# Streaming conformer step on one core: gate-row modulation weights and third taps moved into block 0's attention, more work on ScalarE, zero-padded low part of q in block 0's scores

## The chip, the cores and the metric

One core of one Trainium2 chip runs the whole layer as one program. The metric is the device time of one execution in microseconds. The kernel before takes 1776.56 us, the median of three runs (1776.23 to 1776.82). A profile shows one execution by engine: PE (TensorE, with its weight loads as PEld), DVE (VectorE), ACT (ScalarE), POOL (GpSimd) and SP (SyncE, which here only issues DMAs).

## The reference

One layer over 2048 prompt frames and 32 sample frames, model width 1024, in fp32. In short:

```python
mod = c @ w_mod + b_mod
shift, scale, gate = jnp.split(mod, 3, axis=-1)
h = rms_norm(x, g_pre) * (1 + scale[:, None, :]) + shift[:, None, :]
z = h @ w_in
a, b, z_conv, q, k, v, z_attn, g_conv, g_attn = jnp.split(z, cuts, axis=-1)
u = a * jax.nn.sigmoid(b)
# A: 31-tap causal depthwise convolution of u, LayerNorm over 512 channels
y = jax.nn.silu(layer_norm(y, ln_g, ln_b)) * jax.nn.silu(z_conv)
y_conv = y @ w_conv_out
# B: 8 heads of 64, every 64-frame chunk sees itself and the 8 chunks before
s = q.k * 64 ** -0.5 + bias;  p = softmax(s);  o = p.v
y_attn = (o * jax.nn.silu(z_attn)) @ w_attn_out
merged = sigmoid(g_conv) * y_conv + sigmoid(g_attn) * y_attn
out = rms_norm(merged @ w_o, g_post)
return x + gate[:, None, :] * out
```

The sample frames run the same layer with cached rows in front. `gate` depends on `c` alone, not on a frame; it enters only in the last line.

## The kernel before

**Tiles and blocks.** The prompt is worked in four blocks of 512 frames; block 0 carries the 32 sample frames too, so its rows are 544 wide and its projections come as two halves of 272. Every fp32 operand is split into a high and a low part, and a product is three matmuls (`mm3`: high by high, low by high, high by low). A block has three stretches: the attention (projections of q, k, a, b and the z gates from a list, `FILL`, woven between the score, transpose and value matmuls of 24 units of one pair of heads, one head and one part of the queries); the tail (the two gate projections `C_GC` and `C_GA`, output tile `pj`, and the attention's out projection, `py<-ah`); and the rest (`co`, the convolution's out projection, `py<-cohi`, then `w_o`).

**Weights.** `plan` lists the weight pieces in the order of use, half a megabyte each. `weights()` hands out piece i and splits piece i+2 (ACT copies the high part, L226; DVE or POOL subtracts the low part, L228), has SP load piece i+4 into one of two `raw` buffers, and has ACT issue the 1 MB DMA that keeps piece i+1 in DRAM for the later blocks (L236). Later blocks load the split pieces instead.

**Gate rows.** The eight pieces of `w_mod` for `gate` stand in block 0's tail, one after each pair of gate projections. `gate_rows` loads `b_mod` and `g_post`, accumulates four pieces in one PSUM tile `pm` (L153, four matmuls a piece) and starts `gate_row`, whose `pg` (L583) spreads the row; two DVE operations later it goes to DRAM as `gp_d`, from where the end of the block loads it (`gp`, `gps`).

**Convolution.** The 31 taps of the four channel tiles are 124 DVE operations on `y` a block, taken from one generator, `pace.idle`. In block 0's attention `pace.pump` takes them at fixed places of a unit (`TP`: one at the first, one at the second and none at the third); the others run in the tail, where `pace.tick` takes one whenever the planner's DVE time is at most its PE time plus a lead. After the last tap comes the LayerNorm: `u` sums on POOL, `pmean` twice on PE, rsqrt on DVE, then in `co` the tanh on ACT and `xn` on DVE, and `cohi` and `colo`, which the first `py<-cohi` needs.

**Order.** All engines work in the order written. The planner `Pace` counts PE and DVE time by its own prices and so decides where started tasks and taps are emitted; `on_v` at L227 decides whether DVE or POOL subtracts a low part: DVE for the `mod` pieces, in block 0's tail (`pace.dense`), and where there are no taps left and DVE is ahead.

**Scores.** For a head of 64 rows the high part of q is stored on all 128 rows with the other head's keys' rows (`qh`); its low part `ql` is on 64 rows in block 0, and on 128 rows with zeros in the blocks after it.

Of the kernel before, what the change touches and what calls it, by code (L numbers as in the profile page):

```python
# [8 lines left out]
F32 = mybir.dt.float32  # L9
F32R = mybir.dt.float32r  # L10
# [24 lines left out]
NIN = 5632  # L35
BIG = 1e30
# [9 lines left out]
TP = (1, 1, 0)  # L46
# [5 lines left out]
def FILL(b):  # L52

    part = dict(q=C_Q, k=C_K, a=C_A, b=C_B, z=C_ZA, c=C_ZC)
# [84 lines left out]
def mixer_kernel(ctx, tc, x_prompt, x_sample, c_prompt, c_sample, cache_conv, cache_k, cache_v,  # L139
# [175 lines left out]
    def h_stats(pool, b, xs):  # L315
# [12 lines left out]
        V.tensor_scalar(ss, ss, 1.0 / D, EPS, op0=OP.mult, op1=OP.add)  # L328
# [152 lines left out]
    conv_ready, ln_done = set(), {}  # L481
# [78 lines left out]
    def mod_rows(n, dst):  # L560
        pm = ps.tile([P, 512], F32, tag="T", name="pm", bufs=2)
        for kp in range(KT // 2):
            wh, wl = weights(("mod", 2 * kp, n * 512))
            for kk in range(2):
                k = 2 * kp + kk
                mm(pm[0:4], c4[:, k, :], wh[:, kk, :], k == 0, False)
                mm(pm[0:4], c4[:, k, :], wl[:, kk, :], False, k == KT - 1)
                yield
        V.tensor_copy(dst, pm[0:4])

    def gate_rows(tmp):

        for n in range(2):
            m4, bg = tmp("m4")[0:4, 0:512], tmp("bg")
            bm, gr = bg[0:2, 0:512], bg[0:2, 512:1024]
            nc.sync.dma_start(bm, dram(b_mod, 2 * D + n * 512, [[0, 2], [1, 512]]))
            nc.sync.dma_start(gr, dram(g_post, n * 512, [[0, 2], [1, 512]]))
            yield from mod_rows(4 + n, m4)
            pace.start(gate_row(n, m4, bm, gr), 4.0)

    def gate_row(n, m4, bm, gr):
        pg = pp_tile("pg")
        nc.tensor.matmul(pg[0:2], lhsT=sel, rhs=m4, start=True, stop=True)  # L583
        V.tensor_tensor(bm, pg[0:2], bm, op=OP.add)
        V.tensor_tensor(bm, bm, gr, op=OP.mult)
        nc.sync.dma_start(gp_d[:, n * 512:(n + 1) * 512], bm)
        yield 0.0
# [31 lines left out]
    with tc.tile_pool(name="init", bufs=1) as ini:  # L619
# [64 lines left out]
        with tc.tile_pool(name="x0", bufs=5) as x0:  # L684
# [37 lines left out]
            V.tensor_scalar(ss, ss, 1.0 / D, EPS, op0=OP.mult, op1=OP.add)  # L722
# [74 lines left out]
    for b in range(NB):  # L797
        NT, YW, ypieces = shape(b)
        PTW = 896 if b == 0 else 1280
        TW = TB + TS if b == 0 else 640  # L800
        LA = 2 if b == 0 else 1

        with tc.tile_pool(name="at", bufs=1) as at:
            def tmp(name):
                return at.tile([P, NT], F32, tag="tmp", name=name, bufs=3)
# [29 lines left out]
            if b == 1:  # L835

# [607 lines left out]
```

## Time and profile before

| | us |
|---|---|
| median of three runs | 1776.56 |
| profiled execution | 1774.66 |
| its span | 1772.9 |
| PE busy in the span | 1690.7 (95%) |
| DVE busy | 1154.7 (65%) |
| ACT busy | 597.5 (34%) |
| POOL busy | 212.1 (12%) |

The profiled execution is 1.9 us under the median and 1.8 us longer than its span. PE's share says that the kernel is mostly matmul; it is an average, and the 82 us without PE lie in a few places. In forty slices of the span, the eleventh (443 to 487 us, the end of block 0's tail) has PE busy at half and its granted clock at 0.6 of full; all other slices after the start show 8 or 9 tenths.

### The profile page before, as it was taken

What the parts mean: (1) busy time and instruction counts of PE and PEld (TensorE: products, weight loads), DVE (VectorE), ACT (ScalarE), POOL (GpSimd) and SP (SyncE); (2) the same over time, 40 slices, a digit from 0 to 9 for tenths busy, and PEclk for the clock granted to TensorE, in tenths of its full rate; (3) what the DMA queues carried; (4) which work ended last, traced back from release to release, by engine and by line L of the source; (5) the groups of instructions that cost most, each with busy time, mean ns of one, the idle gap of its engine ahead of it and who ended that gap; (6) DMA issues with size and microseconds to landing.
All of it is one profiled execution on the core that took longest, in us unless ns stands there. A gap on an engine that the chain in (4) does not pass through costs nothing.

```text
span 1772.9 us, 23618 instructions
## 1 busy us (share of the span) xinstructions
PE 1690.7 (95%) x9221; PEld 1430.4 (81%) x9221; DVE 1154.7 (65%) x2119; ACT 597.5 (34%) x1156; POOL 212.1 (12%) x163
## 2 busy tenths in 40 slices
PE   6889999989499999999899999999999999999997
PEld 4778899988388788888788888888888888888886
DVE  6556876887855957775652967765652967766523
ACT  5345454233331245531220035531320045531211
POOL 4322222002220000001120000001120000000120
PEclk9999999999699999999999999999999999999999
DMA  8796565767375684465465585455565574445553
GB/s 267 216 326 207 189 215 202 272 229 262 132 255 196 243 305 174 156 221 190 150 217 188 196 307 188 140 198 210 181 218 191 199 272 144 171 167 201 190 190 143
DMA packets 132326, 368.61 MB, mean 208 GB/s; under 512 B 9326, under 2 KB 75050, under 8 KB 101975
## 3 DMA queue, kind: packets, MB, share of 16 engines
q1 hardware_dynamic: 123575, 304.19, 50.1%
q10 hardware_dynamic: 8640, 62.92, 8.7%
q8 instruction: 73, 1.20, 0.3%
q14 instruction: 38, 0.31, 0.1%
HBM read 280.41 MB, written 91.77 MB: 210 GB/s over the span
## 4 chain that ended last, share of the span: by engine, by line
PE 78%; DVE 8%; DMA 4%; ACT 2%; issue 1%; ACTq 0%; POOL 0%; DVEq 0%; SPq 0%; POOLq 0%
PE pj L153 44%; PE py L153 8%; PE pv L153 4%; PE sps L153 4%; PE pt L157 4%; PE op L153 3%; PE oT L153 3%; PE oS L153 3%; PE oP L153 1%; DVE y L134 1%; DVE w L134 1%; PE vS L153 1%; PE vT L153 1%; DMA raw<-in_w_attn_out_dram 1%; DMA raw<-in_w_in_dram 1%
## 5 line engine op out<-in xcount | busy, mean ns | idle before, releaser
L153 PE MATMUL pj<-hh,w 128*128 128x512 f32 (+1 forms) x4800 | 974.7, 357 | 11.9 <-DVE kk L134 6.1
L153 PEld LDWEIGHTS pj<-hh,w 128*128 128x128 f32 x4800 | 778.4, 189 | 133.2 <-issue 8.9
L134 DVE SCALAR_TENSOR_TENSOR y<-u,dww,y 128x512 f32<-128x512 f32 (+1 forms) x480 | 338.2, 770 | 0.4
L1073 ACT ACTIVATE sp<-sp,mn 128x640 f32<-128x640 f32 (+5 forms) x136 | 103.7, 762 | 112.5 <-DVE mn L134 112.3
L1108 ACT ACTIVATE pth<-pt 128x256 fp32r<-128x256 f32 (+4 forms) x184 | 91.9, 501 | 135.8 <-PE pt L157 129.3
L134 DVE TENSOR_TENSOR ptl<-pt,pth 128x256 fp32r<-128x256 f32 (+4 forms) x184 | 104.2, 567 | 27.2 <-ACT pth L1108 25.4
L134 DVE CUSTOM_DVE_ANT_0 sp<-sps,bias 128x640 f32<-128x640 f32 (+4 forms) x128 | 94.4, 737 | 29.6 <-PE sps L153 28.1
L153 PE MATMUL py<-cohi,w 128*128 128x512 f32 (+1 forms) x320 | 93.5, 366 | 19.2 <-ACT cohi L1260 17.7
L226 ACT ACTIVATE w<-raw 128x1024 fp32r<-128x1024 f32 x72 | 75.6, 1054 | 89.1 <-DMA raw<-in_w_mod_dram 18.6
L153 PE MATMUL py<-ah,w 128*128 128x512 f32 (+1 forms) x480 | 96.3, 356 | 8.3 <-DVE t L134 7.1
L153 PEld LDWEIGHTS py<-ah,w 128*128 128x128 f32 x480 | 80.1, 192 | 23.5 <-DVE t L134 7.5
L157 PE MATMUL pt<-ident,sp 128*128 128x128 f32 (+1 forms) x600 | 94.2, 272 | 0.0
L228 POOL TENSOR_TENSOR w<-raw,w 128x1024 fp32r<-128x1024 f32 x30 | 73.3, 2443 | 170.5 <-ACT w L226 142.8
L528 POOL TENSOR_TENSOR u<-y 128x512 f32<-128x512 f32 (+1 forms) x4 | 6.3, 1581 | 671.4 <-DVE y L134 671.4
L153 PEld LDWEIGHTS py<-cohi,w 128*128 128x128 f32 x320 | 58.8, 195 | 29.0 <-ACT cohi L1260 19.1
L134 DVE TENSOR_SCALAR sp<-sp,ll 128x640 f32<-128x640 f32 (+5 forms) x136 | 75.6, 556 | 4.8
L134 DVE TENSOR_TENSOR w<-raw,w 128x1024 fp32r<-128x1024 f32 x42 | 53.3, 1278 | 31.5 <-ACT w L226 31.0
L153 PE MATMUL sps<-kk,qh 128*128 128x320 f32 (+1 forms) x224 | 69.2, 316 | 3.3 <-DVE kk L134 2.0
L157 PEld LDWEIGHTS pt<-ident,sp 128*128 128x128 f32 (+1 forms) x600 | 68.8, 140 | 3.9 <-issue 1.3
L153 PE MATMUL sps<-kk,ql 128*128 128x320 f32 (+1 forms) x224 | 70.8, 323 | 0.0
L1344 POOL TENSOR_TENSOR mg<-mg,t 128x512 f32<-128x512 f32 (+1 forms) x32 | 46.4, 1451 | 168.7 <-issue 114.0
L134 DVE SCALAR_TENSOR_TENSOR t<-t,py 128x512 f32<-128x512 f32 (+1 forms) x40 | 23.2, 584 | 59.3 <-PE py L153 59.2
(247 smaller groups left out, 2224.8 us busy)
## 6 DMA issues: line engine op xcount, KB each, us to landing
w<-kept SPq DMA_DIRECT2D x176, 1024.0 KB
kept<-w ACTq DMA_DIRECT2D x60, 1024.0 KB
raw<-in_w_in_dram SPq DMA_DIRECT2D x48, 512.0 KB
bias<-bias_d SPq DMA_DIRECT2D x32, 320.0 KB
xt<-in_x_prompt_dram SPq DMA_DIRECT2D x16, 512.0 KB
wm<-in_w_mod_dram SPq DMA_DIRECT2D x16, 512.0 KB
xr<-in_x_prompt_dram SPq DMA_DIRECT2D x16, 512.0 KB
vs_d<-vcur SPq DMA_DIRECT2D x12, 512.0 KB
```

What stands on the lines that cost most here:

```text
L134: return fn(out, *a, **k)
L153: nc.tensor.matmul(out, lhsT=lhsT, rhs=rhs, start=start, stop=stop)
L157: nc.tensor.transpose(out, in_, idn)
L226: act(wh, raw, AF.Copy)
L228: (V if on_v else G).tensor_tensor(wl, raw, wh.bitcast(F32), op=OP.subtract)
L528: G.tensor_tensor(s2[:, 0:YW], Y[2][:, 0:YW], Y[3][:, 0:YW], op=OP.add)
L1073: self.ex[i] = lambda: act(sp[0:m, 0:nk], sp[0:m, 0:nk], AF.Exp, bias=mn[0:m], scale=-1.0, accum_out=ll[0:m])
L1108: act(self.ph[0:r, f0:f1], pt[0:r, o:o + f1 - f0], AF.Copy)
L1344: G.tensor_tensor(mg, mg, t2, op=OP.add)
```

## The change

It touches block 0 most. The eight gate pieces move from the tail's list into the attention's (`m0` to `m7` of `FILL`); each has a PSUM tile of its own, and ACT (first piece) or DVE (the others) adds it to a row in `aof`. `TP` takes a third tap in each unit. `ql` gets 128 rows with zeros in block 0 too. The second form of `h` (`hf`) and the LayerNorm's `xn` are computed by ACT instead of DVE; rsqrt has nine DVE operations instead of eleven, and the division by the width goes into the squares' scale. Scores tiles `sp` become parts of one row, and `tmp` has two buffers instead of three in block 0. The low part of a `mod` piece is now subtracted by whichever engine the planner's rule picks.

```diff
-TP = (1, 1, 0)
+TP = (1, 1, 1)
...
-    order = "b0 a0 q1 k1 b1 a1 b2 q2 k2 a2 z0 b3 a3 z1 q3 k3 z2 z3 c0 c1 c2 c3" if b == 0 else \
+    order = "b0 a0 q1 m0 k1 m1 b1 m2 a1 m3 b2 q2 m4 k2 m5 a2 m6 z0 m7 b3 a3 z1 q3 k3 z2 z3 c0 c1 c2 c3" if b == 0 else \
...
-                on_v = key[0] == "mod" or pace.dense or pace.idle is None and pace.dve <= pace.pe + DV
+                on_v = pace.dense or pace.idle is None and pace.dve <= pace.pe + DV
...
-    def rsqrt(y, x, xh, t, iters=3):
+    def rsqrt(y, x, t, u):
         V.tensor_scalar(y.bitcast(I32), x.bitcast(I32), -0.5, 1597463007.0, op0=OP.mult, op1=OP.add)
-        V.tensor_scalar(xh, x, -0.5, None, op0=OP.mult)
-        for _ in range(iters):
-            V.tensor_tensor(t, y, y, op=OP.mult)
-            V.tensor_tensor(t, t, xh, op=OP.mult)
-            V.scalar_tensor_tensor(y, t, 1.5, y, op0=OP.add, op1=OP.mult)
+        V.scalar_tensor_tensor(t, y, -0.5, y, op0=OP.mult, op1=OP.mult)
+        V.tensor_tensor(t, t, x, op=OP.mult)
+        V.scalar_tensor_tensor(y, t, 1.5, y, op0=OP.add, op1=OP.mult)
+        V.tensor_tensor(t, y, y, op=OP.mult)
+        V.tensor_tensor(t, t, x, op=OP.mult)
+        V.tensor_scalar(u, t, 0.375, -1.25, op0=OP.mult, op1=OP.add)
+        V.tensor_tensor(u, u, t, op=OP.mult)
+        V.scalar_tensor_tensor(y, u, 1.875, y, op0=OP.add, op1=OP.mult)
...
-        V.tensor_scalar(hf, src, Gm[:, w, ct:ct + 1], Sh[:, w, ct:ct + 1], op0=OP.mult, op1=OP.add)
+        act(hf, src, AF.Identity, scale=Gm[:, w, ct:ct + 1], bias=Sh[:, w, ct:ct + 1])
...
+    def mod_part(i):
+        n, kp = i // 4, i % 4
+        m4, bm, gr = aof[0:4, 3, 0:512], aof[0:2, 2, 0:512], aof[0:2, 1, 0:512]
+        if kp == 0:
             nc.sync.dma_start(bm, dram(b_mod, 2 * D + n * 512, [[0, 2], [1, 512]]))
             nc.sync.dma_start(gr, dram(g_post, n * 512, [[0, 2], [1, 512]]))
+        wh, wl = weights(("mod", 2 * kp, (4 + n) * 512))
+        pm = pp_tile("pm")
+        for kk in range(2):
+            mm(pm[0:4], c4[:, 2 * kp + kk, :], wh[:, kk, :], kk == 0, False)
+            mm(pm[0:4], c4[:, 2 * kp + kk, :], wl[:, kk, :], False, kk == 1)
+            yield
+        if kp == 0:
+            act(m4, pm[0:4], AF.Copy)
+        else:
+            V.tensor_tensor(m4, pm[0:4], m4, op=OP.add)
+        if kp == 3:
+            pace.start(gate_row(n, m4, bm, gr), 1.5)
...
-                return at.tile([P, NT], F32, tag="tmp", name=name, bufs=3)
+                return at.tile([P, NT], F32, tag="tmp", name=name, bufs=2 if b == 0 else 3)
...
-            if b == 1:
+            if b < 2:
+                qls.clear()
                 for _ in range(2):
-                    qls.append(wp.tile([P, 2, TB], F32R, tag="raw", name="ql0"))
+                    qls.append(wp.tile([P, 2, TB], F32R, tag="raw", name="ql0") if b else
+                               at.tile([P, 2, NT], F32R, tag="ql", name="ql", bufs=2))
                     G.memset(qls[-1][64:128, 0].bitcast(F32), 0.0)
                     G.memset(qls[-1][0:64, 1].bitcast(F32), 0.0)
...
                 mm(out, qh[:, s, q0:q0 + m], kk[:, s, k0:k1], True, False)
-                if b == 0:
-                    mm(out, ql[r, q0:q0 + m], kk[r, s, k0:k1], False, True)
-                else:
-                    mm(out, ql[:, s, q0:q0 + m], kk[:, s, k0:k1], False, True)
+                mm(out, ql[:, s, q0:q0 + m], kk[:, s, k0:k1], False, True)
...
-            rate = (88.0 if b == 0 else 62.0) / sum(loads)
+            rate = (95.0 if b == 0 else 62.0) / sum(loads)
...
-                        V.tensor_scalar(xn[ct][:, o0:o1], Y[ct][:, a0:a1], vecs[:, 44 + ct:45 + ct],
-                                        vecs[:, 48 + ct:49 + ct], op0=OP.mult, op1=OP.add)
+                        act(xn[ct][:, o0:o1], Y[ct][:, a0:a1], AF.Identity, scale=vecs[:, 44 + ct:45 + ct],
+                            bias=vecs[:, 48 + ct:49 + ct])
```

PE in block 0's tail, the stretch that ends in `co`. `pj` are the gate projections, `py<-ah` the attention's out projection, `pm` and `pg` the gate rows, `pmean` the LayerNorm's sums and `pxt` the transposes of the next block's input. Before, its last rows:

```order
L153 MATMUL pmean<-lnlo,onesr 128x32
L153 MATMUL pj<-hh,w 128x272 x3
L153 MATMUL pm<-w,c_91 4x512 x4
L153 MATMUL py<-ah,w 128x272 x48
L153 MATMUL pm<-w,c_91 4x512 x4
L583 MATMUL pg<-m_4460,sel 2x512
L153 MATMUL pmean<-lnhi,onesr 128x512
L153 MATMUL pmean<-lnlo,onesr 128x512
L153 MATMUL pmean<-lnhi,onesr 128x32
L153 MATMUL pmean<-lnlo,onesr 128x32
L157 MATMUL pxt<-ident,xt 128x128 x4
L153 MATMUL py<-cohi,w 128x272
```

and the changed kernel's PE in the same tail, from the first `pmean` group on:

```order
L155 MATMUL pmean<-lnlo,onesr 128x32
L155 MATMUL pj<-hh,w 128x272 x15
L155 MATMUL py<-ah,w 128x272 x48
L155 MATMUL pj<-hh,w 128x272 x45
L155 MATMUL pmean<-lnhi,onesr 128x512
L155 MATMUL pmean<-lnlo,onesr 128x512
L155 MATMUL pmean<-lnhi,onesr 128x32
L155 MATMUL pmean<-lnlo,onesr 128x32
L155 MATMUL pj<-hh,w 128x272 x147
L155 MATMUL py<-ah,w 128x272 x48
L159 MATMUL pxt<-ident,xt 128x128 x4
L155 MATMUL py<-cohi,w 128x272
```

Before, only the four transposes stand between the second `pmean` group and the first `py<-cohi`; now 147 `pj` and 48 `py<-ah` do, and `pm` and `pg` are gone from the tail.

DVE at the start of that tail, up to the first operation on a `py<-ah` (`t`). `ah` is the attention's output split, `w<-raw` the subtraction of a weight's low part, `y` a tap. Before:

```order
L134 TENSOR_TENSOR ah<-aof,ah 128x544 x4
L134 TENSOR_TENSOR w<-raw,w 128x1024
L134 SCALAR_TENSOR_TENSOR y<-u,dww,y 128x574 x3
L134 TENSOR_TENSOR w<-raw,w 128x1024
L134 SCALAR_TENSOR_TENSOR y<-u,dww,y 128x574 x6
L134 TENSOR_TENSOR w<-raw,w 128x1024
L134 SCALAR_TENSOR_TENSOR y<-u,dww,y 128x574 x2
L134 TENSOR_SCALAR y<-u,dww,vecs 128x574
L134 SCALAR_TENSOR_TENSOR y<-u,dww,y 128x574 x3
L134 TENSOR_TENSOR w<-raw,w 128x1024
L134 SCALAR_TENSOR_TENSOR y<-u,dww,y 128x574 x6
L134 TENSOR_TENSOR w<-raw,w 128x1024 x2
```

and DVE at the same place of the changed kernel:

```order
L136 TENSOR_TENSOR ah<-aof,ah 128x544 x4
L136 TENSOR_TENSOR w<-raw,w 128x1024
L136 SCALAR_TENSOR_TENSOR y<-u,dww,y 128x574 x2
L136 TENSOR_TENSOR w<-raw,w 128x1024
L136 SCALAR_TENSOR_TENSOR y<-u,dww,y 128x574 x6
L136 TENSOR_TENSOR w<-raw,w 128x1024
L136 SCALAR_TENSOR_TENSOR y<-u,dww,y 128x574 x6
L136 TENSOR_TENSOR w<-raw,w 128x1024
L136 TENSOR_SCALAR y<-u,dww,vecs 128x574
L136 SCALAR_TENSOR_TENSOR y<-u,dww,y 128x574 x6
L136 TENSOR_TENSOR w<-raw,w 128x1024
L136 SCALAR_TENSOR_TENSOR t_3576<-t_3576,py 128x272
```

The number of taps ahead of `t` is the same, 21; one of six subtractions is gone.

## Rows read from the trace of the kernel before

**Rows 1.** PE's waits, 310 to 500 us: engine, line, releaser, total us, times, longest.

```profile
PE py L153 <- ACT cohi L1260: 17.7, 4, 13.8
PE py L153 <- DVE t L134: 7.1, 2, 6.2
...
PE py L153 <- DVE mg L134: 1.0, 2, 0.5
PE pxt L157 <- DVE hf L134: 0.7, 1, 0.7
```

**Rows 2.** PE's timeline, block 0's tail: start, busy us, work, count, [idle before].

```profile
300.26 24.32 PE L153 MATMUL pj<-hh,w 128*128 128x272 f32 x192
324.42 1.09 PE L153 MATMUL pm<-w,c 128*4 128x512 f32 x4
325.35 4.67 PE L153 MATMUL py<-ah,w 128*128 128x272 f32 x36
...
369.98 3.09 PE L153 MATMUL py<-ah,w 128*128 128x272 f32 x12 [6.22 <-DVE t L134]
...
446.55 0.80 PE L153 MATMUL pmean<-lnhi,onesr 128*128 128x512 f32 x1
...
462.79 0.59 PE L153 MATMUL py<-cohi,w 128*128 128x272 f32 x1 [13.82 <-ACT cohi L1260]
...
476.25 0.64 PE L157 MATMUL pxt<-ident,xt 128*128 128x128 f32 x4
```

**Rows 3.** PE's timeline at scores: block 0 (256 to 268 us), then block 1.

```profile
256.89 0.40 PE L153 MATMUL sps<-kk,qh 128*128 128x512 f32 x1
...
257.65 3.26 PE L153 MATMUL pj<-hh,w 128*128 128x272 f32 x24
260.75 0.40 PE L153 MATMUL sa<-kk,qh 128*32 128x512 f32 x1
...
261.68 0.55 PE L157 MATMUL pt<-ident,sp 128*128 128x128 f32 x3
...
267.48 0.22 PE L153 MATMUL sps<-kk,qh 128*128 128x128 f32 x1
...
267.89 0.66 PE L157 MATMUL pt<-ident,sp 128*128 128x128 f32 x4
...
705.02 0.31 PE L153 MATMUL sps<-kk,qh 128*128 128x320 f32 x1
...
705.32 0.31 PE L153 MATMUL sps<-kk,qh 128*128 128x320 f32 x1
```

**Rows 4.** Stretches: us, then busy us (instructions) by engine, PE clock, DMA share, GB/s.

```profile
core 0: us, PE busy (x) PEld busy (x) DVE busy (x) ACT busy (x) POOL busy (x), PEclk, DMA share, GB/s
111.40:286.30 174.90, 171.46 (x1285) 154.28 (x1284) 129.91 (x309) 89.30 (x216) 49.12 (x24) 1.00 0.61 212
...
205.78:228.66 22.88, 22.88 (x172) 20.45 (x173) 18.71 (x41) 10.23 (x26) 7.31 (x4) 1.00 0.56 199
300.26:370.00 69.74, 62.42 (x482) 60.00 (x481) 56.81 (x73) 21.30 (x34) 1.92 (x1) 0.98 0.77 268
```

**Rows 5.** Groups by form: attention (two rows, 100 to 300), tail (two, 300 to 432).

```profile
L228 POOL TENSOR_TENSOR w<-raw,w 128x1024 fp32r<-128x1024 f32 x22 | 54.2, 2463 | 139.8 <-ACT w L226 112.2 <-DMA kept<-w 7.5 <-DMA raw<-in_w_in_dram 5.3
L134 DVE SCALAR_TENSOR_TENSOR y<-u,dww,y 128x574 f32<-128x574 f32 x40 | 36.2, 906 | 0.1
...
L134 DVE SCALAR_TENSOR_TENSOR y<-u,dww,y 128x574 f32<-128x574 f32 x80 | 60.8, 812 | 0.3
L134 DVE TENSOR_TENSOR w<-raw,w 128x1024 fp32r<-128x1024 f32 x25 | 31.6, 1272 | 23.7 <-ACT w L226 23.2 <-issue 0.4
```

**Rows 6.** ACT's waits, 300 to 448 us.

```profile
ACT w L226 <- DMA raw<-in_w_mod_dram: 18.6, 3, 7.1
```

**Rows 7.** PE's longest wait on DVE before 310 us, and ACT's timeline ahead of it.

```profile
PE pj L153 <- DVE kk L134: 6.1, 1, 6.1
...
95.67 0.39 ACT L855 ACTIVATE kk<-pj 64x272 fp32r<-64x272 f32 x1 [5.58 <-DMA bias_d<-msk]
```

**Rows 8.** PE's longest wait after 500 us.

```profile
PE pj L153 <- DVE t L134: 4.5, 1, 4.5
```

More of the change, by code (lines that the diff above doesn't have):

```diff
@@ L35 @@
 NIN = 5632
+C_MOD = -1
 BIG = 1e30
@@ L52, in FILL @@
 def FILL(b):
-    part = dict(q=C_Q, k=C_K, a=C_A, b=C_B, z=C_ZA, c=C_ZC)
-    order = "b0 a0 q1 k1 b1 a1 b2 q2 k2 a2 z0 b3 a3 z1 q3 k3 z2 z3 c0 c1 c2 c3" if b == 0 else \
+    part = dict(q=C_Q, k=C_K, a=C_A, b=C_B, z=C_ZA, c=C_ZC, m=C_MOD)
+    order = "b0 a0 q1 m0 k1 m1 b1 m2 a1 m3 b2 q2 m4 k2 m5 a2 m6 z0 m7 b3 a3 z1 q3 k3 z2 z3 c0 c1 c2 c3" if b == 0 else \
         "q1 k1 z0 q2 k2 z1 q3 k3 z2 z3 c0 c1 c2 c3"
@@ L182, in w_half, with w_fill @@
         return ((name, m), 2 * P, lambda r: (r, src[0, :, m * P:(m + 2) * P].rearrange("(k p) c -> p k c", p=P)))
-    mods = [w_wide("mod", w_mod, k, n * 512) for n in (4, 5) for k in range(0, KT, 2)]
+    def w_fill(n, col):
+        return w_wide("mod", w_mod, 2 * (n % 4), (4 + n // 4) * 512) if col == C_MOD else w_cols(col + n * P)
     for b in range(NB):
         plan += [w_wide("v", w_in, k, C_V) for k in range(0, KT, 2)]
-        plan += [w_cols(c + n * P) for n, c in [(0, C_Q), (0, C_K)] + FILL(b)]
+        plan += [w_fill(n, c) for n, c in [(0, C_Q), (0, C_K)] + FILL(b)]
         for m in range(0, KT, 2):
@@ L327, in h_stats @@
         t2 = pool.tile([P, 8], F32, tag="ru", name="ru", bufs=2)
[L328 removed]
+        V.tensor_scalar(ss, ss, EPS, None, op0=OP.add)
         rsqrt(rr, ss, t1, t2)
@@ L478, in conv_rows @@
         nc.sync.dma_start(dst[0, 0], us[0:HIST, 0:512])
-    conv_ready, ln_done = set(), {}
+    conv_ready, ln_done, gate_done = set(), {}, set()
     def shape(b):
@@ L558, in norm_conv @@
         ln_done[b] = True
[L560 to L575, printed above, removed]
+    def mod_part(i):
+        n, kp = i // 4, i % 4
+        m4, bm, gr = aof[0:4, 3, 0:512], aof[0:2, 2, 0:512], aof[0:2, 1, 0:512]
+        if kp == 0:
             nc.sync.dma_start(bm, dram(b_mod, 2 * D + n * 512, [[0, 2], [1, 512]]))
             nc.sync.dma_start(gr, dram(g_post, n * 512, [[0, 2], [1, 512]]))
-            yield from mod_rows(4 + n, m4)
-            pace.start(gate_row(n, m4, bm, gr), 4.0)
+        wh, wl = weights(("mod", 2 * kp, (4 + n) * 512))
[10 more added lines that the diff above has]
+            pace.start(gate_row(n, m4, bm, gr), 1.5)
     def gate_row(n, m4, bm, gr):
@@ L583, in gate_row @@
         nc.tensor.matmul(pg[0:2], lhsT=sel, rhs=m4, start=True, stop=True)
+        yield 1.5
         V.tensor_tensor(bm, pg[0:2], bm, op=OP.add)
@@ L586, in gate_row @@
         nc.sync.dma_start(gp_d[:, n * 512:(n + 1) * 512], bm)
+        gate_done.add(n)
         yield 0.0
@@ L799, in mixer_kernel @@
         PTW = 896 if b == 0 else 1280
-        TW = TB + TS if b == 0 else 640
+        TW = PTW if b == 0 else 640
         LA = 2 if b == 0 else 1
@@ L847, in qk_alloc @@
                 qh = at.tile([P, 2, NT], F32R, tag="qh", name="qh", bufs=2)
-                ql = at.tile([P, NT], F32R, tag="ql", name="ql", bufs=2) if b == 0 else qls[hp % 2]
-                att[hp] = [kk, None, qh, ql]
+                att[hp] = [kk, None, qh, qls[hp % 2]]
                 if b:
@@ L882, in sink_q @@
                         act(qh[64 - 64 * s:128 - 64 * s, s, c0:c1], o[r], AF.Copy, scale=-0.125)
-                        V.scalar_tensor_tensor(ql[r, c0:c1] if b == 0 else ql[r, s, c0:c1], o[r], -0.125, qh[r, s, c0:c1].bitcast(F32),
+                        V.scalar_tensor_tensor(ql[r, s, c0:c1], o[r], -0.125, qh[r, s, c0:c1].bitcast(F32),
                                                op0=OP.mult, op1=OP.subtract)
@@ L941, in sink @@
                 def sink(o, c0, c1):
+                    assert len(gate_done) == 2 or key == ("za", 0)
                     tz = tmp("tz")
@@ L951, in mixer_kernel @@
                     C_B: lambda n: b_proj(b, n), C_A: lambda n: a_proj(b, n, tmp),
+                    C_MOD: mod_part,
                     C_ZA: lambda n: z_proj(C_ZA + n * P, aof[:, n], ("za", n)),
@@ L1039, in score @@
                         load_bias(2 * hp + s + 1)
-                    sp = self.sp[i] = at.tile([P, TW], F32, tag="sp", name="sp", bufs=2 + 2 * LA)
+                    if b:
+                        sp = self.sp[i] = at.tile([P, TW], F32, tag="sp", name="sp", bufs=2 + 2 * LA)
+                    else:
+                        if i == 0:
+                            self.row = at.tile([P, TW], F32, tag="sp", name="sp", bufs=1 + LA)
+                        sp = self.sp[i] = self.row[:, 0:TB + TS] if g == 2 else self.row[:, i * self.nk[0]:i * self.nk[0] + self.nk[i]]
                     mn = at.tile([P, 1], F32, tag="mm", name="mn", bufs=8)
@@ L1293, in mixer_kernel @@
             xs = []
-            gr = gate_rows(lambda name: tl_.tile([P, D], F32, tag="x", name=name, bufs=XB)) if b == 0 else None
             for m2 in range(0, KT, 2):
@@ L1302, in mixer_kernel @@
                     pace.run(proj(C_GA + m * P, b, lambda o, c0, c1: act(t2[:, c0:c1], o, AF.Tanh, scale=0.5)))
-                    if gr and m:
-                        for i in range(2):
-                            next(gr, None)
-                            pace.tick()
                 wa = weights(("ao", m2))
@@ L1311, in mixer_kernel @@
                         t2[:, c0:c1], t2[:, c0:c1], 1.0, o, op0=OP.add, op1=OP.mult)))
-            if gr:
-                for _ in gr:
-                    pace.tick()
             while pace.idle is not None:
```

17 lines of the change are left out of this document (6 added, 11 removed).

## The prediction

> **What bounds the kernel now.** I read the page's busy shares first: PE has 95% of the span, so a change can only pay where PE waits, runs at the lower clock, or has fewer cycles to spend. The slices then say where that is: nearly everywhere 8 or 9 tenths, and one hole at 443 to 487 us with the clock at 0.6. PE's waits around it [rows 1] name the hole: 17.7 us on `cohi`, 13.8 of them in one piece, and 7.1 on DVE's `t`. The timeline [rows 2] shows why: the second `pmean` starts at 446.55, the first `py<-cohi` at 462.79, and between them the LayerNorm's chain (rsqrt on DVE, `y` on POOL, tanh on ACT, `xn`, `cohi`) runs with PE empty. The chain is late because the taps are: block 0's tail holds 82 of its 124. The stretches [rows 4] show what else is tight: DVE is busy 129.91 of 174.90 us in the attention, and 56.81 of 69.74 in the tail's first half. Two smaller waits on PE stand elsewhere: 6.1 us on `kk` near 96 us [rows 7] and 4.5 us in block 1 [rows 8].
>
> **The change part by part.** I sum in the profiled execution, 1774.66 us, which lies 1.9 us under the median.
>
> *Block 0's tail.* From its first `pj` (300.26) to the second `pxt` (476.25), 175.99 us [rows 2]. What PE still has to do there: 16 gate pieces and 4 out pieces of 48 matmuls each, 960 in all. 192 take 324.42 − 300.26 = 24.16 us, so 960 take 120.8; the `pmean` groups and transposes are worth about 2, the first 24 matmuls on `cohi` 3.0. That is 125.8 us without a wait. The chain of 16.2 us (446.55 to 462.79) now has 195 matmuls = 24.5 us over it by the order, so it is hidden even if nothing in it gets shorter; with xn moved to ACT and two rsqrt operations fewer it should not grow either. The last of the four `cohi` comes later than the first (17.7 − 13.8 us of waits), which may leave a microsecond.
> What is next late is DVE. Up to the first `t` of the second `py<-ah` group, DVE has 49 taps before as after, and 10 weight subtractions instead of 13: 56.81 − 3 × 1.27 = 53.0 us of work [rows 4, 5]. PE needs 192 + 48 + 192 + 36 = 468 matmuls, 58.9 us, to get there. DVE idled 12.9 us of this stretch before, mostly for weights that had not arrived (23.7 us by 432) [rows 4, 5]. Five fit in the 58.9; with 10 of 13 pieces left I expect about 10 idle, so a stall of 4 us, and one more for the third group. Bounds: 0 if the loads come in time, 12 if DVE idles as before and the third group waits too. Tail: 125.8 + 5 = 130.8, that is **−45** (−50 to −38).
>
> *Scores in block 0.* With `ql` on 64 rows a pair of matmuls takes 257.65 − 256.89 = 0.76 us at 512 columns and 267.89 − 267.48 = 0.41 at 128; on 128 rows two matmuls of 320 take 0.30 [rows 3], in proportion 0.48 at 512 and 0.12 at 128. So 0.28 to 0.29 a pair, whatever the width: switching costs it, not columns. 32 pairs give 9.0 us; the eight sample scores take 261.68 − 260.75 = 0.93 and should take 0.60, another 2.6. **−11.6**. The zeros are set by four POOL memsets at the start of the attention, where POOL has room.
> The rows say that 64 rows cost more. The Trainium skill says the opposite for an operand of this size: for a contraction of 64 or less, page "TensorEngine Tiling (Array Packing)", section "When to Use Tiling", advises row tiling, with up to twice the speed. By that rule padding would save nothing here, and this term would be 0; the same page's "Key Properties" says that changing the tiling mode drains the engine, and with that the trace agrees.
>
> *Gate pieces in the attention.* Eight pieces of four matmuls, 0.93 us each (324.42 to 325.35) [rows 2], 7.4 us, and the two `pg`, which I price like one piece: **+8.3** on PE, since PE is nearly full there (171.46 of 174.90 us) [rows 4]. In the tail they were counted out above.
>
> *DVE in the attention.* 21 more taps at 0.906 = 19.0 us, and ten small operations for the gate rows, 6 to 7 us by their 512 columns against a tap's 574 [rows 5]. 129.91 + 26 = 156 us [rows 4]. PE there: 171.5 + 8.3 − 10 = 170. So DVE goes from 74% to 92% of the time in which PE would not wait. The nearest row is the pass at 205.78, where DVE had 18.71 of 22.88 (82%) and PE not one wait [rows 4]; scores run two units ahead, which absorbs waits of a microsecond. Bounds: 0, and, if DVE can't pass 82%, 156/0.82 = 190, +20. I take **+5**, nearer to the first since the tail ran DVE at 81% with weights as its only trouble.
> The subtractions that move to POOL (7 of the 8, by the order) take 2.46 us each and stretch taps beside them: a tap takes 0.906 in the attention with 22 of them, 0.812 in the tail [rows 5], 40 × 0.094 = 3.8 us or 0.17 for each; 7 more are 1.2 us, in the 5. The Trainium skill, page "SBUF — State Buffer", section "SBUF: two separate sides", has a harder rule: a DVE operation with two SBUF inputs and a GpSimd operation that reads SBUF exclude each other for a whole instruction. By that, seven subtractions would block DVE for up to 17 us more, a rival below. The rows bear out a part of it only.
>
> *Start of the kernel.* The `kk` copies on ACT stood 5.58 us behind a DMA that ACT had to issue and that waited for the mask's write; PE lost 6.1 us [rows 7]. With the zeros and the queue's new order that issue waits for an older transfer. Against this, sixteen `hf` operations move from DVE to ACT in the input stretch. **−3** (−7 to +2).
>
> *Small ones.* `hf` and `mg` waits at the transposes (1.7 us) go, since DVE has eight operations fewer there [rows 1]: −1.6. The 4.5 us in block 1 [rows 8] shorten with the rsqrt chain; between 0 and −4.5 I take −2.5. The end of the kernel and later blocks, nine for eleven rsqrt operations: −0.8.
>
> Sum: −45 − 11.6 + 8.3 + 5 − 3 − 1.6 − 2.5 − 0.8 = −51.2. 1774.7 − 51.2 = 1723.5 in the profile; +1.9 gives a median of **1725.4**.
>
> **The rivals.** The times are medians.
> A: *DVE becomes the attention's bound.* The third tap and the gate rows push it past what it reached anywhere; POOL's subtractions block it. For it: 92% against 82% [rows 4]. Against it: two units of lead. +20 instead of +5: 1740.
> B: *The tail stays late.* ACT waits for raw weights (three waits of 6 us on `mod` alone) [rows 6], DVE's subtraction stands behind six taps, and the loads of `gp`, `gps` and the residual now come early too. DVE idles as much as before: stalls of 12 instead of 5, plus 5 in later pieces: 1737. With A, 1752.
> C: *The zeros do nothing*, as the change says they should: 128 rows cost what 64 do, because the switch is not what the rows measure. 1725.4 + 11.6 = 1737.
> D: *Slower than before.* The gate pieces now follow each other at every second place of the attention's list. Each is used in 0.93 us, so the piece after it must be loaded and split in the time of one; ACT works in order, and behind its copy of a weight that hasn't landed stand the exponentials, `pth` and `qh`, for which PE waits. If each of the eight cost PE 7 us (the 7.1 of rows 6 in full), 56 us, the gain is gone: 1781. It decides from 6.4 us a piece on. Against it: DMA is busy 61% in the attention against 77% in the tail [rows 4], and pieces are loaded four ahead.
> E: everything hides, the attention at 0, the tail at −50, the start at −7: 1711.
>
> **How the numbers follow.** Forecast, 1717 to 1733: 0.50. A alone 0.14, B alone 0.13, C 0.07, A with B 0.06, E 0.06, D 0.04. The likeliest is the forecast, 1725.4. From E to A with B all but 2 in 10 should lie between 1708 and 1748. A measurement of this kernel can tell about 0.2% (3.6 us) from no change. Only D, and a mild form of it, reaches that band: faster 0.94, same 0.02, slower 0.04.
>
> **What would show it.** In the changed profile: the timeline of the tail has no `py<-cohi` wait over 2 us, and its `pj` to second `pxt` takes 126 to 138 us; the pair of scores at 512 columns takes about 0.48 and at 128 about 0.12; PE's waits from 110 to 300 us sum to under 10; a tap's mean in the attention stays under 1.0. Wrong it is if PE's waits on `mn`, `pth`, `ptl` or `kk` in the attention exceed 15 us (A or D; in D the releaser behind them is ACT's `w` after a raw load), if `t` holds `py<-ah` for 10 us or more (B), or if the score pairs are as before (C).

## The result and the profile after

The changed kernel takes 1753.11 us (median of four runs, 1752.31 to 1753.47) against 1776.69 us for the kernel before (four runs): a ratio of 0.9864, 95% interval 0.9847 to 0.9881. It is 24 us faster, where 51 were forecast, and outside the range. The profiled execution has a span of 1750.5 us, 22.4 less than before.

On the page PE is busy 1676.9 us, so its idle time fell only from 82 to 74 us.

The stretches say where the forecast held. Columns as in [rows 4]. The first row is the attention's passes two to five (a pass is one head, three units, and ends with the last `pvs<-vsam`), the second the tail from its first `pj` to the second `pxt`:

```profile
133.13:251.85 118.72, 99.86 (x686) 86.91 (x687) 95.12 (x197) 53.42 (x124) 40.83 (x18) 0.91 0.56 188
...
326.27:461.07 134.80, 127.69 (x998) 126.46 (x997) 106.97 (x154) 55.28 (x95) 19.43 (x14) 0.99 0.75 267
```

and the same two of the kernel before:

```profile
134.94:228.66 93.72, 91.35 (x679) 81.30 (x680) 70.94 (x175) 47.68 (x117) 25.36 (x13) 1.00 0.56 195
...
300.26:476.25 175.99, 144.90 (x1033) 133.72 (x1033) 142.41 (x201) 58.52 (x93) 19.53 (x14) 0.89 0.66 229
```

The tail went from 176.0 to 134.8 us, -41.2, close to the forecast. But it starts at 326.27 instead of 300.26: everything ahead of it is 26.0 us longer, where -1.3 was forecast. Nearly all of that (25.0) is in the four passes. What follows the tail is 7.2 us shorter.

The tail's timeline of the changed kernel answers to [rows 2]: the hole of 13.82 us is gone, the first `py<-cohi` follows `pxt` at once, and what waits is small.

```profile
358.24 3.06 PE L155 MATMUL py<-ah,w 128*128 128x272 f32 x12 [3.17 <-DVE t L136]
...
457.62 0.60 PE L159 MATMUL pxt<-ident,xt 128*128 128x128 f32 x4
457.98 0.37 PE L155 MATMUL py<-cohi,w 128*128 128x272 f32 x1
...
461.07 0.60 PE L159 MATMUL pxt<-ident,xt 128*128 128x128 f32 x4
```

In passes two to five PE has waits that the kernel before did not have; there they were two of 1.0 us on `kk` and one of 0.3 us. Now they are (engine, line, releaser, total us, times, longest):

```profile
PE pj L155 <- DVE kk L136: 4.4, 1, 4.4
PE pg L587 <- DVE aof L136: 3.7, 1, 3.7
PE pm L155 <- DVE ql L136: 2.2, 1, 2.2
PE po L159 <- DVE aof L136: 2.0, 1, 2.0
PE pj L155 <- ACT u L446: 2.0, 1, 2.0
```

and four kinds more, all on DVE, that sum to 4.4 us. The first wait in PE's timeline, and the same kind of matmuls in a later pass:

```profile
140.43 1.70 PE L155 MATMUL pj<-hh,w 128*128 128x272 f32 x6 [4.42 <-DVE kk L136]
...
304.97 0.96 PE L155 MATMUL pj<-hh,w 128*128 128x272 f32 x6
```

Behind the wait, the matmuls are slow: six `pj` took 1.70 us, against 0.96 in the last row. The granted clock of the four passes is 0.91 of full, where it was 1.00: for part of the time TensorE ran at 1.2 instead of 2.4 GHz, which costs about 0.09 x 118.7 = 10.7 us. PE's idle time there rose from 2.4 to 18.9 us.

### The profile page after: what moved, and what is told of

It reads as the page before. It is cut to its first block, busy times and chain, and to the rows that moved or that the text cites. A ratio compares the mean times of both kernels' runs of the same rounds, so it can differ in the third digit from the quotient of the medians.

```text
span 1750.5 us, 23607 instructions
## 1 busy us (share of the span) xinstructions
PE 1676.9 (96%) x9221; PEld 1428.5 (82%) x9221; DVE 1122.5 (64%) x2030; ACT 633.5 (36%) x1218; POOL 234.6 (13%) x174
## 4 chain that ended last, share of the span: by engine, by line
PE 73%; DVE 4%; ACT 2%; DMA 1%; issue 1%; POOL 0%; POOLq 0%; ACTq 0%; DVEq 0%
PE pj L155 41%; PE py L155 9%; PE pv L155 4%; PE op L155 3%; PE sps L155 3%; PE pt L159 3%; PE oT L155 3%; PE oS L155 3%; PE vS L155 2%; PE vT L155 2%; PE oP L155 1%; DMA raw<-in_w_in_dram 1%; DVE pre L136 1%; DMA raw<-in_w_attn_out_dram 1%; PE pxt L159 0%
## 5 line engine op out<-in xcount | busy, mean ns | idle before, releaser
L136 DVE SCALAR_TENSOR_TENSOR y<-u,dww,y 128x512 f32<-128x512 f32 (+1 forms) x480 | 345.9, 781 | 0.5
L136 DVE TENSOR_TENSOR ptl<-pt,pth 128x256 fp32r<-128x256 f32 (+4 forms) x184 | 104.0, 565 | 28.1 <-ACT pth L1119 26.7
L228 POOL TENSOR_TENSOR w<-raw,w 128x1024 fp32r<-128x1024 f32 x37 | 92.2, 2497 | 177.3 <-ACT w L226 147.7
L155 PEld LDWEIGHTS py<-ah,w 128*128 128x128 f32 x480 | 79.8, 192 | 20.5 <-DVE t L136 5.2
L136 DVE TENSOR_SCALAR sp<-sp,ll 128x640 f32<-128x640 f32 (+5 forms) x136 | 84.5, 621 | 4.8
L1311 ACT ACTIVATE t<-pj 128x512 f32<-128x512 f32 (+1 forms) x40 | 20.7, 517 | 127.6 <-PE pj L155 127.4
L136 DVE SCALAR_TENSOR_TENSOR t<-t,py 128x512 f32<-128x512 f32 (+1 forms) x40 | 23.2, 584 | 67.1 <-PE py L155 67.0
```

What stands on the lines that cost most here:

```text
L136: return fn(out, *a, **k)
L155: nc.tensor.matmul(out, lhsT=lhsT, rhs=rhs, start=start, stop=stop)
L228: (V if on_v else G).tensor_tensor(wl, raw, wh.bitcast(F32), op=OP.subtract)
L1311: pace.run(proj(C_GC + m * P, b, lambda o, c0, c1: act(t1[:, c0:c1], o, AF.Tanh, scale=0.5)))
```

## The experiments

What is compared is the time of passes two to five ("the passes") and of the tail. Single runs are set against the changed kernel's 1753.1; the kernel before took 1778.6 beside the first seven, 1776.7 to 1778.4 beside the others.

How far one run can be trusted shows in the kernel of e16, which was profiled twice: its passes took 109.5 and 108.3 us, its tail 134.8 and 136.5, its pass one ended at 134.96 and at 138.78, and its five times lie between 1743.99 and 1749.74. So 1 to 2 us in a stretch, 4 ahead of pass two and 6 in a total of one run say nothing by themselves.

Theory T was that the third taps do it, P that POOL's subtractions block DVE, G and R that the gate pieces hold PE by their place or their PSUM buffer, D that DVE simply has more to do than fits (rival A). Later S is P again, with a price for POOL's hold on DVE.

**e1: two taps again.**

```diff
-TP = (1, 1, 1)
+TP = (1, 1, 0)
```

> The changed kernel with the third tap of a unit taken back (TP 1, 1, 0); all else as in the changed kernel. In the changed kernel the passes two to five of the attention (133.1 to 251.9 us) take 118.7 us where they took 93.7, with PE's clock at 0.88 to 0.94. Theory T (taps): the third taps push DVE over what the attention holds. Then these passes shrink to 96 to 102 us, the clock there is back at 1.00, and the tail loses its cover (in the order the second pmean stands right ahead of the first py on cohi): +16 to +20 us. Total 1750 to 1757. Theory P (the gate pieces' subtractions on POOL block DVE): the passes stay over 112 us and the total goes to 1763 to 1775. Theory G (the gate rows' own small DVE operations and their place in PE's order hold PE): the passes stay over 108 us.

1759.4 us.

```profile
132.72:242.42 109.70, 96.48 (x687) 84.33 (x687) 84.15 (x186) 54.34 (x126) 40.16 (x18) 0.95 0.60 204
...
315.02:468.14 153.12, 131.16 (x998) 127.86 (x998) 119.95 (x173) 55.91 (x95) 17.18 (x14) 0.92 0.66 235
```

The passes lost 9.0 us with 11 us of DVE work, but they are still 16 us over the kernel before, which has as many taps. The tail grew by 18.3, as expected: its hole on `cohi` (12.8 us) is back. T explains a third of the 25.0 and missed its range (96 to 102), P missed too; "over 108", which G expected, is what came.

**e2: gate pieces subtracted on DVE.**

```diff
-                on_v = pace.dense or ...
+                on_v = key[0] == "mod" or pace.dense or ...
```

> The changed kernel with the gate pieces' low parts subtracted on DVE, as before the change, instead of on POOL. T: DVE gets 8 x 1.27 = 10 us more in the attention and is the bound there, so passes two to five grow from 118.7 to 122 to 128 us; total 1756 to 1763. P: POOL's 7 subtractions of 2.5 us no longer lengthen DVE's operations; passes two to five shrink to 105 to 112 us, total 1740 to 1747.

1765.4 us.

```profile
139.76:259.20 119.44, 99.28 (x686) 86.83 (x687) 98.56 (x203) 53.49 (x124) 25.87 (x12) 0.91 0.55 186
```

POOL is back at the level of before (25.9 us) and the passes are no shorter: neither theory's range was met. Which of the two engines does it makes no difference there; what the run lost, it lost ahead of pass two (+6.6 us) and in the tail (+4.8).

**e3: the low part of q on 64 rows.**

```diff
-                mm(out, ql[:, s, q0:q0 + m], kk[:, s, k0:k1], False, True)
+                mm(out, ql[r, q0:q0 + m], kk[r, s, k0:k1], False, True)
```

(for block 0 alone, with `ql` stored as before the change)

> The changed kernel with the low part of q on 64 rows again in block 0's scores. The prediction's price of the zeros is 11.6 us of PE time. If PE is still what the attention waits for: total +11 to +12, 1764 to 1765. T (DVE is the bound in passes two to five): four of eight passes hide PE's saving, total +4 to +8, 1757 to 1761. If the zeros save nothing: 1752 to 1754.

1759.2 us.

```profile
136.48:254.54 118.06, 104.14 (x686) 86.39 (x687) 94.26 (x195) 52.98 (x123) 40.81 (x18) 0.93 0.54 184
```

The most telling run: PE is busy 4.3 us longer in the passes, and they are no longer than with the zeros. PE is not what sets their length. The total is T's; the zeros are worth some 6 us by it, which is no more than one run can be off.

**e4: the kernel before with a third tap.**

```diff
-TP = (1, 1, 0)
+TP = (1, 1, 1)
```

> The kernel before with one edit, the third tap of a unit (TP 1, 1, 1). The tail's order then puts 150 pj and 48 py between the second pmean and the first py on cohi, so the 13.8 us wait and the half clock behind it go: -18 to -22. T: passes two to five grow from 93.7 to 104 to 112 us, total 1764 to 1774. P or G: with no gate piece in the attention the passes stay under 98 us, total 1754 to 1760.

1766.4 against 1778.6 us beside it, 12.2 faster by this one line.

```profile
136.81:233.75 96.94, 92.89 (x680) 82.80 (x680) 80.86 (x185) 46.12 (x114) 25.98 (x13) 0.98 0.53 186
```

Ten more us of DVE work cost the passes 3.2; DVE stands at 83% there. The tail took 160.7 us and lost its hole (-15.3, short of the 18 expected). The passes are as P and G had them (under 98), so T falls as the main cause; the total alone would have fitted T.

**e5: the pieces' PSUM tiles elsewhere; e6: drains first; e9: no additions.**

```diff
-        pm = pp_tile("pm")
+        pm = ps.tile([P, 512], F32, tag="T", name="pm", bufs=2)
```

(and `pg` in the same way)

> The changed kernel with the gate pieces' PSUM tiles pm and pg taken from the two buffers of the transposes (tag T) instead of the three that the projections rotate through. Nothing else moves: the same matmuls, taps, drains and POOL work. Theory R (ring): a gate piece fills one of three projection buffers for 0.93 us of PE work, so the projection after it finds its buffer not yet drained by DVE or ACT, which stand behind taps; PE stops, and its clock falls. Then passes two to five shrink from 118.7 to 99 to 107 us, the clock there is 0.97 or more, the total is 1734 to 1743. Theory D (rival A of the prediction: DVE has more work than the time holds): DVE's work is the same, the passes stay over 114 us, the total over 1748.

```diff
+        pace.flush()
         pm = pp_tile("pm")
```

> The changed kernel with one line: the deferred drains of the projections are written out before a gate piece takes its PSUM tile, so that they stand earlier in DVE's and ACT's order. R: most of the waits for a projection's buffer go, passes two to five 102 to 112 us, total 1738 to 1748. D: no change within 3 us of 1753.

```diff
         if kp == 0:
             act(m4, pm[0:4], AF.Copy)
-        else:
-            V.tensor_tensor(m4, pm[0:4], m4, op=OP.add)
```

> The changed kernel without the six DVE additions of the gate pieces (left out: three of four pieces never reach the gate row), so a gate piece's PSUM tile is free as soon as PE is done with it, but still takes its turn among the three. D: 4 us of DVE work less, passes two to five 113 to 116 us, total 1748 to 1751. R: the projection after the next no longer waits for the addition, but the turn that the piece takes still brings the others' drains forward by one: passes 104 to 112 us, total 1739 to 1748. If the place in the ring alone did it, no change.

e5: 1752.9 us, passes 118.4. The wait of 4.42 us on `kk` for a buffer became one of 3.14 us on `kk` itself (`sps<-kk`): the data was late, not the buffer. R falls. e6: 1750.2 us, passes 111.7 as R had them, but the end of pass one came 4.9 us later and the total is D's; little of it is a gain. e9: 1743.0 us, passes 108.1: without 4 us of additions DVE's busy time fell by 4.3 and the passes by 10.7. These are R's numbers and not D's, though e5 had taken R's ring away; e11 below, which moves the additions elsewhere, did not repeat the total.

**e10: no low parts of the gate pieces.**

```diff
-                (V if on_v else G).tensor_tensor(wl, raw, wh.bitcast(F32), op=OP.subtract)
+                if key[0] != "mod":
+                    (V if on_v else G).tensor_tensor(wl, raw, wh.bitcast(F32), op=OP.subtract)
```

> The changed kernel without the subtraction of the gate pieces' low parts (left out: the gate rows use the high part twice, PE's work is the same). POOL loses its 7 additional subtractions of 2.5 us and DVE the one that it had. Theory S (shared access): while POOL subtracts, a DVE operation that meets it is held until it ends; moving the subtraction to DVE (run e2) only swapped 6.5 us of held operations for 9 us of DVE work. Without either, DVE's busy time in passes two to five falls from 95.1 to 87 to 90 us, the passes from 118.7 to 104 to 111, the total to 1739 to 1747. If POOL's subtractions cost DVE only what the prediction said (0.17 us each, 1.2 in all): passes over 115, total over 1749.

1750.9 us.

```profile
134.33:248.13 113.80, 98.44 (x687) 86.50 (x687) 89.94 (x199) 53.49 (x124) 26.59 (x12) 0.93 0.58 195
```

DVE's busy time fell by 5.2 us though no operation of its own went in these passes: POOL has six subtractions less there, so each had held DVE for 0.9 us. The mean times of the same operations account for 3.6 of it (2.2 on the four `sp<-sp,ll` of 384 columns, which take 1.33 us in the changed kernel and 0.79 here, 0.8 on `vh`, 0.6 on the taps), or 0.6 each. The passes fell by 4.9, to between both expectations; DVE's time is that of S, the total (over 1749) that of the small price. How the holding works can be seen in the changed kernel's timelines of DVE and of POOL:

```profile
226.25 1.96 DVE L136 SCALAR_TENSOR_TENSOR aof<-oo,aof 128x544 f32<-128x544 f32 x1
228.13 2.89 DVE L136 SCALAR_TENSOR_TENSOR y<-u,dww,y 128x574 f32<-128x574 f32 x1
230.95 0.67 DVE L136 TENSOR_TENSOR aof<-pm,aof 4x512 f32<-4x512 f32 x1
```

```profile
225.25 5.17 POOL L228 TENSOR_TENSOR w<-raw,w 128x1024 fp32r<-128x1024 f32 x2 [4.24 <-ACT w L226]
```

POOL runs two subtractions back to back from 225.25 to 230.42. Beside them DVE works at two operations that take 0.73 and 0.80 us when alone: the first ends at 228.21, 0.6 us after the first subtraction (227.63 in the trace), the second at 231.02, 0.6 us after the second. And the gate piece's addition, for which `pg` waits 3.72 us, stands behind them.

**e11 and e12: the sum of the pieces on PE; and fewer third taps.** ACT copies each piece to partitions of its own, and one matmul with a taller `sel` adds and spreads them:

```diff
-        if kp == 0:
-            act(m4, pm[0:4], AF.Copy)
-        else:
-            V.tensor_tensor(m4, pm[0:4], m4, op=OP.add)
+        act(aof[32 * kp:32 * kp + 4, 3, 0:512], pm[0:4], AF.Copy)
```

> A full kernel: the changed one, with the four pieces of a gate row copied by ACT to four groups of partitions and added by the pg matmul that spreads the row anyway, so DVE's six additions of 0.67 us are gone and nothing takes their place on PE. Theory D (DVE behind PE, each catch-up wait paid again in clock): as in run e9, passes two to five 106 to 111 us, total 1741 to 1747. If it is the pieces' place in PE's order and not DVE's work: no gain, 1751 to 1755.

e12 also takes the third tap only in units 0 to 2 and from 9 on:

> As e11, and no third tap in the units of passes two and three (six taps go to the tail). D: those passes lose 5 to 6 us of DVE work and shrink by 4 to 8 together; in the tail 105 pj and 48 py (19 us) still stand between the second pmean and the first py on cohi, over a chain of 16, so the tail grows by 0 to 2. Total 1736 to 1743. If taps cost nothing there, as in run e4: within 2 us of e11.

e11: ratio to before 0.9847 (0.9832 to 0.9862), 1750.4 us, passes 111.6 with DVE at 89.6. e12: 0.9846 (0.9826 to 0.9865), passes 110.8 with DVE at 85.6, tail 138.0. Both fell short: 5.6 us of DVE work gave 7.1, the next 4.0 gave 0.7, which is nothing clear. So DVE's sum is not all of it. The waits of 4.42 us on `kk` and 1.97 us on `u` stood in e10 and e11 to the hundredth as in the changed kernel.

**e13: the gate pieces back in the tail,** all other edits kept (list, `gate_rows`, `on_v` and `rate`, how fast the list is worked off, as before the change).

```diff
-    order = "b0 a0 q1 m0 k1 m1 b1 m2 a1 m3 b2 q2 m4 k2 m5 a2 m6 z0 m7 b3 a3 z1 q3 k3 z2 z3 c0 c1 c2 c3" if b == 0 else \
+    order = "b0 a0 q1 k1 b1 a1 b2 q2 k2 a2 z0 b3 a3 z1 q3 k3 z2 z3 c0 c1 c2 c3" if b == 0 else \
```

> The changed kernel with the gate pieces back in the tail, as before the change; zeros, third taps, the work on ACT and the scores' rows stay. D (DVE's work sets the length of passes two to five): their DVE work is that of run e4 (81 us), so they take 93 to 99 us instead of 118.7; the tail is that of e4 (160.7 us) less the shorter rsqrt: 155 to 161 instead of 134.8. Total 1748 to 1756. If another edit in the attention (zeros, two tmp buffers, the rows of scores) holds these passes: over 106 us and a total over 1762.

1751.0 us.

```profile
132.05:225.54 93.49, 87.82 (x680) 82.84 (x680) 80.25 (x182) 46.67 (x115) 25.82 (x13) 0.96 0.56 195
...
296.88:456.72 159.84, 142.64 (x1032) 134.31 (x1032) 118.04 (x165) 62.68 (x102) 17.99 (x14) 0.95 0.68 235
```

This shows which edit it is. Without the pieces the passes take 93.5 us, third taps, zeros and all; with them 118.7. Set beside e1 and e4 it shows how the two loads add: the pieces with two taps cost 16.0 us (109.7 against 93.7), the third tap without pieces 3.2, both 25.0, so some 6 come only from the two together. The tail starts 29.4 us earlier and takes 25.0 longer, and the total is that of the changed kernel within 2 us. The move of the gate pieces, the largest edit, is worth nothing that one run can tell.

**e14, e15, e16: other places in the list** (sum on PE and drains first in all three).

```diff
-b0 a0 q1 m0 k1 m1 b1 m2 a1 m3 b2 q2 m4 k2 m5 a2 m6 z0 m7 b3 a3 z1 q3 k3 z2 z3 c0 c1 c2 c3
+b0 a0 q1 k1 b1 a1 b2 q2 k2 m0 a2 m1 z0 m2 b3 m3 a3 m4 q3 m5 k3 m6 c0 m7 z1 z2 z3 c1 c2 c3
```

> A full kernel: the changed one with the sum of a gate row's pieces on PE (as e11), the drains written out ahead of a piece (as e6), and the pieces later in the list: the first after k2, the last before z1, so none stands in passes two and three and most in four to seven. D: passes two and three take 47 to 51 us together instead of 58.3, passes four and five 50 to 56 instead of 60.4, pass six up to 2 more; the tail stays within 2 us of 134.8. Total 1733 to 1743. If the pieces cost the same wherever they stand: 1746 to 1752.

(e15 has "b1 m0 a1 b2 m1 q2 k2 m2 a2 z0 m3 b3 m4 a3 m5 q3 m6 k3 m7 z1" in its middle; e16 the list of the changed kernel.)

> As e14, but with the pieces spread from the first pass to the seventh, one after every second other piece. D: no pass holds more than one or two; passes two to five 104 to 110 us, total 1738 to 1747.

> As e14, with the list of the changed kernel: the sum on PE and the drains ahead alone. D: passes two to five 106 to 110 us, total 1743 to 1749. Against e14 it tells what the place in the list is worth.

e14: ratio 0.9837 (0.9808 to 0.9866), 1748.5 us. Passes two and three took 45.2 us, even less than expected, all four 98.7; but pass one ended 4.0 us later, and the list also moved projections on: pass eight has 170 matmuls instead of 111 and took 20.5 us instead of 13.1 without PE ever idle. Passes two to eight together took 182.3 us, against 192.2 in the changed kernel. e15: 1760.8 us, a miss: the passes took 104.0, but passes six to eight took 88.7 instead of 73.5. e16: 1746.1 us in one run, passes 109.5, tail from 319.4. It has e14's other two edits and the changed kernel's list, and its passes two to eight took 183.5 us: against e14's 182.3 the place in the list gains nothing, as the second expectation had it.

**e17, e18: drains ahead of the weights' split, for gate pieces (against e16 the line moves up) and for all; e16 again.**

```diff
+        pace.flush()
         wh, wl = weights(("mod", 2 * kp, (4 + n) * 512))
```

> As e16, but the projections' drains are written out ahead of the call that splits the next weight piece, so that ACT's copies of kk, qh and u stand before its 1.05 us copy of a weight instead of behind it. If the waits at the starts of passes two, three and four (3.1, 2.0 and 3.4 us in e16, on kk and u) are a matter of this order: each 1 us shorter, the clock over 0.96 there, passes two to five 102 to 107 us, total 1739 to 1744. If the chain ahead of them (mn from DVE, then the exponentials on ACT) sets them: within 2 us of e16, 1744 to 1748.

> As e17, and ahead of every projection's weight in block 0, not only the gate pieces'. Order theory: another 2 to 4 us less, total 1737 to 1742. Chain theory: no gain, or up to 4 us more, since drains now stand ahead of the scores' normalisation on DVE.

> Run e16 timed: 1746 if its one look holds, so 5 to 9 us under the changed kernel's 1753.1.

e17: 1747.2 us; the wait on `kk` at the start of pass two shrank to 0.2 us, and one of 3.07 us on `mn` took its place eight us earlier. e18: 1749.4 us, with 3.08 on `mn` there. The passes of e17 took 104.2, in the range of the order theory, but its pass one ended at 141.16, 2.4 us later than in e16's second run, for the new wait lies in it. The totals are the chain theory's: the same lateness shows at the next thing that PE needs. e16 again: 1748.7 us, ratio 0.9822 (0.9788 to 0.9856). It is faster than the kernel before; against the changed kernel's 0.9864 (0.9847 to 0.9881) the intervals overlap, so it isn't shown to beat it.

## Why the prediction was wrong

**The step that failed is the term for DVE in the attention** (+5, between 0 and +20). With the gate pieces, the zeros and the start the sum came to -1.3 up to the tail; measured was +26.0. By e13, which has the third taps and the zeros but not the pieces, passes two to five are 25.2 us longer with the pieces, and 20.2 of that are waits of PE and the clock lost with them, in place of the 5. Rival A (chance 0.14) comes nearest, and even its +20, which makes +13.7 up to the tail, was short. The parts, passes two to five of the changed kernel against e13:

- PE idle: 18.9 against 5.7 us, +13.2.
- Clock: 0.91 of 118.7 against 0.96 of 93.5, 10.7 against 3.7 us lost, +7.0. The prediction priced waits in the attention at their own length and no more, though the hole in block 0's tail had shown that matmuls behind a wait run at half rate.
- The pieces' own PE work: 28 matmuls at 0.93 us per four and two `pg` at the same price, +8.4. The +8.3 for it was rightly sized.
- By the counts 26 other matmuls fewer (21 of them projections), at the 0.126 us of a projection's: -3.3, an estimate (they fell into other passes).

Together 25.3, against 25.2 measured.

What PE waits for is DVE: 16.7 of the 18.7 us of waits in these passes end with one of its operations, 2.0 with one of ACT's. But DVE is not full there. It is busy 95.1 of 118.7 us, and it waits itself, most of all for ACT (17 us), and ACT for DVE's `mn` (32.8 us): a loop through both engines, in which each step comes late. So rival A is right in the engine and only in part in its reason, that DVE has more work than fits. The prediction took DVE from 74% to 92% of the time in which PE would not wait. DVE does not reach 92%: its share of the passes was 76% before, 83% in e4 and 86% in e13, and PE's idle time grew with it, 2.4, 4.1 and 5.7 us; with gate pieces the share lay between 77% and 85%, and only with the drains ahead of the weight's split (e17, e18) at 88% and 89%, in passes still of 104 and 106 us. The lowest of these, 77% in e1, has 13.2 us of idle PE, so 82% without a wait [rows 4] was no row to go by: the share alone does not tell how long PE waits. In e3 4.3 us of PE work cost nothing, which is the same from the other side. Of the prediction's signs, PE's waits from 110 to 300 us sum to 23.2 us where it asked for under 10; a tap's mean stayed under 1.0 (0.984 in the passes).

**Rival D** (weights that have not landed) is seen in one place only, in pass one: ACT stands 6.86 us behind a raw load up to 97.32, the exponentials and DVE behind it, and PE waits 6.74 us on `mn`. From 110 to 300 us ACT waits for no load in the changed kernel, so D is not what lengthens passes two to five.

**The 0.17 us for a subtraction on POOL was too small by three to five times.** It came from the mean of taps, 0.906 against 0.812 [rows 5], spread over 22 subtractions. But other operations than taps are held as well, and e10 gives 0.6 to 0.9 us each (3.6 to 5.2 us for six). The Trainium skill's page "SBUF — State Buffer" ("SBUF: two separate sides") has an exclusive lock between the two engines for the whole instruction. The timelines of DVE and POOL under e10 agree with the mechanism: in both cases the operation that met a subtraction ended 0.6 us after it. The size is a quarter to a third of the 2.5 us; that DVE is not always at such an operation is the likely reason, but no run shows it.

**The tail held.** 125.8 us without waits and a stall of 5 were forecast, 130.8; measured 134.8, with 7.1 us of waits in it, the first on `t` 3.17 (4 forecast), and PE's busy time at 127.7. The chain of the LayerNorm is covered, as the order showed. But the reason given for the gain, the pieces and the taps together, splits unlike it read: by e1 the third taps' cover is worth 18.3 of the tail, by e13 the pieces' removal 25.0, and only the former is cheap in the attention, and only without the pieces (3.2 in e4, 9.0 by e1).

**The zeros** do what was said. In the changed kernel a pair of scores takes 0.17 us at 128 columns and 0.47 at 512 (155.06 to 155.53), and the sample's scores 0.53 (287.27 to 287.80), where 0.12, 0.48 and 0.60 were forecast and 0.41, 0.76 and 0.93 stood before [rows 3]:

```profile
294.74 0.22 PE L155 MATMUL sps<-kk,qh 128*128 128x128 f32 x1
...
294.91 0.62 PE L159 MATMUL pt<-ident,sp 128*128 128x128 f32 x4
```

This does not speak against tiling rows, as the prediction read it: the kernel before works one matmul of 64 rows at a time between those of 128, and whether two at once would be faster no run shows. Some 6 of the 11.6 us reach the end by e3, which is one run; its passes show why not all do, since PE is not their bound. A saving on PE and a load on DVE in the same stretch were added up as if PE were the bound for both.

**The rest.** Block 1's wait on `t` went from 4.5 [rows 8] to 2.4 us (-2.1, forecast -2.5). After the tail the kernel is 7.2 us shorter, forecast 4.9 (1.6, 2.5 and 0.8). The start gave -1.8 by the end of pass one; the wait on `kk` [rows 7] fell to 1.0 as expected, but the 6.7 us on `mn` came after it, so the -3 was right in sign and lost most of its size there.

**What stays open.** DVE's busy time does not set the passes alone: with the pieces early in the list they take 109 to 111 us whether DVE has 84 (e1), 86 (e12) or 87 (e16), 104 to 106 spread out or with drains first at 88 to 94 (e15, e17, e18), and 93 to 99 without them or with them later, at 80 to 84 (e13, e4, e14). Some 10 us thus belong to how the pieces stand between projections, in a chain through ACT and DVE that no single wait names; e5, e6, e17 and e18 show that it is neither the buffer nor the order of drains alone. That the pieces do it is shown; by which of their steps (ACT's copy of the weight, POOL's hold, the additions, the turn on PE) is shown only in part.

## What to carry to other kernels

Before work is moved under other work, ask of the new place which engines' loop sets its length; a stretch where PE is 97% busy can be one that its feeding engines are about to set, and then PE savings there hide, and an added step can cost three times its own length (8.4 us of pieces here, 25.2 in all), in waits and in the clock lost behind them. Do not take a feeding engine's busy share as the gauge: here PE waited 13 us at a share of 77% (e1) and 6 at 86% (e13). Try such a move by itself before its gain is summed with others. Price what one engine does to another (POOL to DVE) over all operations of the second, from its busy time with and without, not from the mean of one kind.

## What the runs showed of the hardware

In passes two to five PE idled 18.9 us in 119, in waits of at most 4.4 us, and the granted clock of the stretch was 0.91, about 10.7 us more, over half of what the waits themselves cost; in e13 5.7 us of idle PE went with 0.96, in the kernel before 2.4 with 1.00. Six POOL subtractions of 2.5 us cost DVE 3.6 to 5.2 us. And a pair of a 128-row and a 64-row matmul took PE 0.41 us at 128 columns and 0.76 at 512, where two of 128 rows took 0.17 and 0.47.
